# Gate and value projections by Strassen's seven products, in a transformer block whose weights stream through one core

## The chip, the cores and the metric

One core of a Trainium2 (trn2) chip runs the whole program. The metric is the device time of one execution in microseconds (us). Names used below: TensorE (PE) multiplies, VectorE (DVE) and ScalarE (ACT) work on tiles in the on-chip memory (SBUF) and on the accumulators (PSUM), GpSimd (POOL) and SyncE (SP) here hardly do more than start transfers from and to DRAM.

## What is computed

One layer of a decoder block on 256 positions of width 2048, in float32:

```python
h = rmsnorm(x, norm_g)
proj = einsum('bsd,df->bsf', h, w_in)          # 2048 -> 18432, cut into 14 pieces
(a_q, a_k, a_v, a_g, b_a, b_b, b_g, c_u, c_v, c_g, d_q, d_k, d_v, d_g) = split(proj)
ya = stick_breaking_attention(a_q, a_k, a_v) * silu(a_g)       # 8 heads of 128
yb = conformer_conv(b_a, b_b, ...) * silu(b_g)                 # gated, 31 taps, layer norm, silu
yc = spatial_gating(gelu(c_u), gelu(c_v), ...) * silu(c_g)     # layer norm, 128x128 mixing
yd = dilated_mixture(d_q, d_k, d_v) * silu(d_g)                # 8 heads, 3 patterns
yproj = einsum('bsnc,ncd->bsnd', [ya, yb, yc, yd], w_branch)   # 1024 -> 2048 each
gates = sigmoid(einsum('bsd,df->bsf', h, w_gate) + b_gate)     # 2048 -> 4 x 2048
merged = sum(gates * yproj, branch)
out = rmsnorm(x + merged @ w_out, final_g)
```

## The kernel before

All weights lie in DRAM as tiles of 128 x 2048 floats (1 MB), in the order of use; `load_weights` takes the next one through SP's queue into one of three `st` buffers. A float32 product is made of three matmuls in TensorE's rounded format: ScalarE copies the tile to `hi` in that format, VectorE subtracts to get the rest, `lo` (`split`, lines L130 and L131, in halves of 1024 columns, five buffers each of `hi` and `lo`), and hi·hi, hi·lo, lo·hi are added up in PSUM. The normed input stands in SBUF all the time as `xhl`, its hi beside its lo.

Two forms of projection use this. `mm_t` gives a transposed result (128 columns of the projection by 256 positions): for each of 16 slices of the depth one matmul of 512 columns (`xhl` hi and lo side by side) and one of 256 (L245, L248). `mm_n` gives positions by 512 columns: 24 matmuls of 512 columns for each tile (L286 to L288). `proj_t` does two transposed tiles (a unit) and evacuates them: ScalarE copies one half, VectorE adds the other (L266, L267).

The work goes: d_v and the norm of x (`make_h`); b_a and b_b; the eight heads of d, where `conv` puts the 248 steps of the convolution ("taps", L412) behind the units as filler; `conv_norm`; then for each branch in the order d, b, a, c the function `gate_proj`: four times, sixteen tiles of the branch's gate (two times 512 columns in PSUM `psg`, with a bias matmul, four tiles a chunk), a sigmoid, and two tiles of the branch's projection (`psy`), multiplied and added to `merged` in SBUF. Between the gates stand the units of b_g, of a (a_v, heads) and of c (c_v, c_u with c_g). At the end `out`.

What must wait for another engine is put off: `later(n, fn)` puts a step on a list, `tick()`, at the end of each unit, counts down and runs those due. So the scores of a head stand behind the next unit, its softmax's transposes behind the one after, then its values; `flush` empties the list. A branch's result `y` is kept in SBUF, as hi and lo (`put_y`).

The order of instructions on every engine is set by the framework's scheduler, which starts from the code's order and moves instructions by priority: weight splits by `SPLIT_AHEAD` = 300 ahead, taps by 100 back.

## Time and profile before

| | |
|---|---|
| median of 3 runs | 1505.48 us (1505.38 to 1506.88) |
| profiled execution | 1508.27 us, span of its profile 1506.6 us |
| mean granted clock of TensorE | 0.994 |
| TensorE matmuls busy | 1479.1 us, 98% of the span |
| VectorE busy | 944.4 us, 63% |
| ScalarE busy | 760.2 us, 50% |
| GpSimd busy | 10.2 us, 1% |
| read from DRAM / written | 277.18 MB / 2.10 MB, 185 GB/s over the span |
| weight tiles loaded whole through SP | 254 of 1 MB, median 4.8 us each |

The busy time of an engine is the time in which it has an instruction at work; in the rows of a line a name such as `lo<-st,hi` says what is written from what, with buffer numbers left out. VectorE's busy share is an average: the page's forty slices go from 4 tenths to 9.

The program by time: to 50 us d_v and the norm; to 145 b_a and b_b; to 506 the heads of d; to 610 the gate and projection of d; then b_g and the gate of b; from about 640 a_v and the heads of a; the gate of a from 1017; c from 1120; the gate of c from 1270; `out` from 1406.

### The profile page before, as it was taken

To read this page: it belongs to the slowest core of one execution; us is meant where nothing else is said; L and a number is where in the kernel's file an instruction comes from. 1 tells how busy PE (TensorE), PEld (TensorE's weight loads), DVE (VectorE), ACT (ScalarE), POOL (GpSimd) and SP (SyncE) were. 2 spreads that over 40 slices of the span, in tenths; PEclk is the share of its full clock that TensorE was granted. 3 is DMA by queue.
4 is the path that set the end of the run, shared out by engine and by line. 5 is a ranking of instruction groups with operands and counts; after the bars stand their busy time and mean duration, and the time that the engine had idled before them with its cause. 6 is when DMAs were issued, how large, how long until landed. Compare 5 with 4: busy or idle time off the path is not lost.

```text
span 1506.6 us, 18648 instructions
## 1 busy us (share of the span) xinstructions
PE 1479.1 (98%) x7484; PEld 1255.4 (83%) x7484; DVE 944.4 (63%) x1249; ACT 760.2 (50%) x860; POOL 10.2 (1%) x22
## 2 busy tenths in 40 slices
PE   7999999999999999999999999999999999999997
PEld 5888888888888788888888888887888888888786
DVE  8899999866566754555545455554545666555454
ACT  7644445564454644454444466654444667444352
POOL 0000000000000000000000000000000000000000
PEclk9999999999999999999999999999999999999999
DMA  8555554445444555555555545444555555555562
GB/s 302 211 195 184 180 187 177 169 166 191 173 168 170 201 203 186 192 195 189 186 186 195 194 168 172 168 177 154 196 195 195 181 183 198 200 190 177 192 217 84
DMA packets 41318, 280.47 MB, mean 186 GB/s; under 512 B 4784, under 2 KB 4784, under 8 KB 8592
## 3 DMA queue, kind: packets, MB, share of 16 engines
q1 hardware_dynamic: 38880, 272.00, 50.5%
q0 software_dynamic: 1632, 6.24, 1.3%
q8 instruction: 58, 0.95, 0.3%
q10 hardware_dynamic: 720, 1.06, 0.2%
q14 instruction: 28, 0.23, 0.0%
HBM read 277.18 MB, written 2.10 MB: 185 GB/s over the span
## 4 chain that ended last, share of the span: by engine, by line
PE 97%; ACT 1%; DVE 1%; DMA 1%; issue 0%; DVEq 0%; ACTq 0%
PE ps L245 30%; PE ps L248 15%; PE psg L286 8%; PE psg L288 8%; PE psg L287 8%; PE psy L286 4%; PE psy L288 4%; PE psy L287 4%; PE psn L287 3%; PE psn L288 3%; PE psn L286 3%; PE pso L286 2%; PE pso L287 2%; PE pso L288 2%; DMA xt<-in_xT_dram 0%; PE psg L369 0%
## 5 line engine op out<-in xcount | busy, mean ns | idle before, releaser
L131 DVE TENSOR_TENSOR lo<-st,hi 128x1024 fp32r<-128x1024 f32 (+1 forms) x506 | 616.0, 1219 | 460.7 <-ACT hi L130 459.2
L130 ACT ACTIVATE hi<-st 128x1024 fp32r<-128x1024 f32 (+1 forms) x506 | 533.4, 1056 | 671.7 <-PE ps L245 262.3
L245 PE MATMUL ps<-xhl,hi 128*128 128x512 f32 x1920 | 675.5, 398 | 0.0
L248 PE MATMUL ps<-xhl,lo 128*128 128x256 f32 x1920 | 519.5, 281 | 0.0
L245 PEld LDWEIGHTS ps<-xhl,hi 128*128 128x128 f32 x1920 | 355.2, 188 | 74.6
L248 PEld LDWEIGHTS ps<-xhl,lo 128*128 128x128 f32 x1920 | 362.3, 189 | 9.6
L286 PE MATMUL psg<-hi,xhl 128*128 128x512 f32 x512 | 201.0, 393 | 1.1 <-ACT hi L130 1.1
L288 PE MATMUL psg<-hi,xhl 128*128 128x512 f32 x512 | 200.3, 391 | 0.0
L287 PE MATMUL psg<-lo,xhl 128*128 128x512 f32 x512 | 200.2, 391 | 0.0
L286 PEld LDWEIGHTS psg<-hi,xhl 128*128 128x128 f32 x512 | 96.4, 188 | 21.6 <-ACT hi L130 1.7
L288 PEld LDWEIGHTS psg<-hi,xhl 128*128 128x128 f32 x512 | 96.6, 189 | 20.2
L287 PEld LDWEIGHTS psg<-lo,xhl 128*128 128x128 f32 x512 | 96.6, 189 | 20.0
L412 DVE SCALAR_TENSOR_TENSOR cv<-glu,vec_sb,cv 128x255 f32<-128x255 f32 (+26 forms) x240 | 100.8, 463 | 0.2
L286 PE MATMUL psy<-hi,y 128*128 128x512 f32 x256 | 99.6, 389 | 0.0
L287 PE MATMUL psy<-lo,y 128*128 128x512 f32 x256 | 99.6, 389 | 0.0
L288 PE MATMUL psy<-hi,y 128*128 128x512 f32 x256 | 99.6, 389 | 0.0
L288 PEld LDWEIGHTS psy<-hi,y 128*128 128x128 f32 x256 | 48.1, 188 | 10.0
L287 PEld LDWEIGHTS psy<-lo,y 128*128 128x128 f32 x256 | 48.1, 188 | 10.0
L286 PEld LDWEIGHTS psy<-hi,y 128*128 128x128 f32 x256 | 48.1, 188 | 9.9
L286 PE MATMUL psn<-hi,xhl 128*128 128x512 f32 x128 | 49.8, 389 | 0.0
L287 PE MATMUL psn<-lo,xhl 128*128 128x512 f32 x128 | 49.8, 389 | 0.0
L288 PE MATMUL psn<-hi,xhl 128*128 128x512 f32 x128 | 49.8, 389 | 0.0
(207 smaller groups left out, 1105.2 us busy)
## 6 DMA issues: line engine op xcount, KB each, us to landing
st<-in_w_dram SPq DMA_DIRECT2D x254, 1024.0 KB, 4.8
xr<-in_x_dram POOLq DMA_DIRECT2D x8, 256.0 KB, 3.9
xt<-in_xT_dram SPq DMA_DIRECT2D x3, 512.0 KB, 8.7
st<-in_w_dram SPq DMA_DIRECT2D x4, 256.0 KB, 5.3
st<-in_w_dram SPq DMA_DIRECT2D x2, 512.0 KB, 7.4
fg<-in_final_g_dram POOLq DMA_DIRECT2D x1, 1024.0 KB, 6.8
out_dram<-r SPq DMA_DIRECT2D x4, 256.0 KB, 3.2
out_dram<-r ACTq DMA_DIRECT2D x4, 256.0 KB, 3.5
```

The source lines that it names most:

```text
L130: A.activation(hi, src, AF.Copy)
L131: V.tensor_sub(lo, src, hi.bitcast(F32))
L245: T.matmul(ps[:, j, :], hi[:, o:o + P], rhs[:, k, :], start=start, stop=stop)
L248: T.matmul(ps[:, j, 0:S], lo[:, o:o + P], rhs[:, k, 0:S], start=False, stop=False)
L286: T.matmul(ps[:, tb, :], lh(k0 + kk, 0, tb), hi[:, o:o + 512], start=st, stop=False)
L287: T.matmul(ps[:, tb, :], lh(k0 + kk, 0, tb), lo[:, o:o + 512], start=False, stop=False)
L288: T.matmul(ps[:, tb, :], lh(k0 + kk, 1, tb), hi[:, o:o + 512], start=False, stop=sp)
L412: V.scalar_tensor_tensor(dst, src, wc, dst, op0=ALU.mult, op1=ALU.add)
```

## The change

Strassen's algorithm (in its form with 15 additions) multiplies two matrices cut in 2 x 2 blocks with seven block products instead of eight, for some additions of blocks beforehand and of products after. Here the left matrix is the normed input, cut in two halves of 128 positions and two of 1024 of depth; its four sums `s1`, `s2`, `s3`, `n4` are made once (`make_sx`) and split to hi and lo. The right one is a piece of 2048 x 1024 of a gate's weights, or the whole of a_v's or c_v's. `group` makes seven products of two half products each; a half product is one weight tile with twelve matmuls of 512 columns into one PSUM bank (`X`, `Z`, `Y`). Sums of weight tiles are made on VectorE before the split (`add_to`, eight to a group). A group loads twelve tiles, four of them for the second time, in place of eight. There are eight groups for the gates and two for values.

A group is a generator: `step(n)`, called between the weight tiles of other units, runs the next n half products of the first group in `queue`. Gate d and a_v's groups run beside the last head of d and the units of b_g, those of gates b and a beside branch d and the units of a, c_v and gate c beside branches b and a and the units of c. A gate's result goes to DRAM (`g_dr`) after its sigmoid and comes back in `branch`, the remaining half of `gate_proj`. The results `y` (`y_dr`) and the merged sum (`m_dr`) go through DRAM too. Each y is loaded back whole through SP's queue (`yf`) and split there.

Weight tiles are split whole, 2048 wide, into three `hi` and two `lo` buffers; there are six `st` buffers. And TensorE no longer follows the scheduler (`manual_schedule`): its instructions stand in the order of the code. The other engines are still scheduled, with `SPLIT_AHEAD` = 100.

```diff
-SPLIT_AHEAD = 300
+SPLIT_AHEAD = 100
...
-    st_p = ctx.enter_context(tc.tile_pool(name="st", bufs=3))
-    sp_p = ctx.enter_context(tc.tile_pool(name="sp", bufs=5))
...
+    st_p = ctx.enter_context(tc.tile_pool(name="st", bufs=6))
+    hi_p = ctx.enter_context(tc.tile_pool(name="hi", bufs=3))
+    lo_p = ctx.enter_context(tc.tile_pool(name="lo", bufs=2))
+    so_p = ctx.enter_context(tc.tile_pool(name="so", bufs=5))
+    ps_x = ctx.enter_context(tc.tile_pool(name="psx", bufs=1, space=bass.MemoryType.PSUM))
+    ps_n = ctx.enter_context(tc.tile_pool(name="psn", bufs=2, space=bass.MemoryType.PSUM))
+    ps_t = ctx.enter_context(tc.tile_pool(name="pst", bufs=3, space=bass.MemoryType.PSUM))
...
+    ctx.enter_context(tc.manual_schedule(engines={mybir.EngineType.PE}))
...
     def tick():
...
         for fn in due:
-            fn()
+            with tc.high_priority(SPLIT_AHEAD):
+                fn()
...
     def make_h():
...
-        pp = ps_2.tile([P, 2, 512], F32, tag="a2", name="pp")
-        pst, psn = pp[:, 0, :], pp[:, 1, :]
+        pst = ps_s.tile([P, 512], F32, tag="s", name="pst")
+        psn = ps_s.tile([P, 512], F32, tag="s", name="psn")
...
+    def proj_t(e0, e1, funcs=(None, None), n=0):
+        dst = qk_p.tile([P, 2, S], F32, tag="qk", name="dst")
+        for j, e in enumerate((e0, e1)):
+            ps = ps_t.tile([P, 512], F32, tag="t", name="ps")
+            mm_t(ps, next_weights(e), xhl)
...
+            step((n + 1) // 2 if j == 0 else n // 2)
+        tick()
+        return dst
...
+    def make_sx():
+        def quarter(k0, t0, name):
+            q = st_p.tile([P, KB, P], F32, tag="st", name=name)
...
...
+        V.tensor_sub(a22[:], a21[:], a22[:])
+        put("s1", a22[:])
+        V.tensor_sub(a22[:], a22[:], a11[:])
+        put("s2", a22[:])
...
+    def group(expect, sink, bias=None):
...
+        def half(ps, st, name, j, first, last):
+            lh = x_part(name)
+            hi, lo = split_tile(st)
+            for kk in range(4):
+                k, o = 4 * j + kk, kk * 512
+                for i, (part, w_) in enumerate(((0, hi), (0, lo), (1, hi))):
+                    T.matmul(ps[:], lh(k, part), w_[:, o:o + 512], start=first and j == kk == i == 0,
...
+        def add_to(st, other):
+            with tc.high_priority(SPLIT_AHEAD):
+                V.tensor_add(st[:], st[:], other[:])
...
+        X = ps_x.tile([P, 512], F32, tag="x", name="X")
...
+        for j in range(2):
+            ts.append(tile_of(0, 0, j))
+            half(X, ts[j], "a11", j, bias is None, True)
+            yield
+        p1 = keep(X, "p1")
+        Z = ps_n.tile([P, 512], F32, tag="n", name="Z")
...
+        for j in range(2):
+            add_to(ts[j], tile_of(1, 0, j))
+            half(Z, ts[j], "s1", j, bias is None, True)
+            yield
+        p5 = keep(Z, "p5")
+        for j in range(2):
+            add_to(ts[j], tile_of(1, 1, j))
+            half(X, ts[j], "s2", j, False, True)
+            yield
+        u2 = keep(X, "u2")
+        for j in range(2):
+            t3, b22 = tile_of(1, 0, j), tile_of(1, 1, j)
+            add_to(t3, b22)
+            half(Z, b22, "n4", j, False, True)
+            yield
+            half(X, t3, "s3", j, False, True)
...
+        Y = ps_n.tile([P, 512], F32, tag="n", name="Y")
+        for j in range(2):
+            b21 = tile_of(0, 1, j)
+            add_to(ts[j], b21)
+            half(Y, b21, "a12", j, True, True)
+            yield
+            half(X, ts[j], "a22", j, False, True)
...
+        done(0, 0, V.tensor_add, Y, p1, p1)
+        done(1, 0, None, X, X, X)
...
+    def put_y(b, h, n, src):
+        nc.gpsimd.dma_start(y_dr[b][:, h:h + n, :], src)
+
+    def branch(b, first=False, sink=None, n=0):
+        yf = st_p.tile([P, 2048], F32, tag="st", name="yf")
+        nc.sync.dma_start(yf[:], y_dr[b][:].rearrange("p k t -> p (k t)"))
+        yhl = [phase(n, F32R) for n in ("yh", "yl")]
+        with tc.high_priority(SPLIT_AHEAD):
+            split(yhl[0][:], yhl[1][:], yf[:])
...
+        for c in range(4):
+            psy = n_banks(1 if queue else c, "psy")
+            for q in range(2):
+                mm_n(psy, next_weights(("brN", bi, c, q)), 4 * q, y_lh, q == 0, q == 1)
+                step(n)
+            tick()
+            for tb in range(2):
+                nc.gpsimd.dma_start(g[:], g_dr[bi, tb, :, o:o + 512])
+                V.tensor_mul(g[:], psy[tb][:], g[:])
...
+                    nc.gpsimd.dma_start(m[:], m_dr[tb, :, o:o + 512])
+                    V.tensor_add(g[:], g[:], m[:])
+                if sink is None:
+                    nc.gpsimd.dma_start(m_dr[tb, :, o:o + 512], g[:])
...
+    for h0 in range(0, NH, 2):
+        sg = proj_t(ft("d_g", h0), ft("d_g", h0 + 1), (AF.Silu, AF.Silu))
+        conv(8)
+        if h0 == 6:
+            conv(len(taps))
+            conv_norm()
+            queue += [gate_group("d", 0), gate_group("d", 1), v_group("a_v", AF.Copy)]
+        d_head(h0, sg, 0)
+        d_head(h0 + 1, sg, 6 if h0 == 6 else 0)
...
+        bg = proj_t(ft("b_g", i), ft("b_g", i + 1), (AF.Silu, AF.Silu), n=6)
...
     for h0 in range(0, NH, 2):
         a_pair(h0)
+    while queue:
+        step()
+        tick()
+    while pending:
+        tick()
+    queue += [v_group("c_v", AF.Gelu_apprx_tanh), gate_group("c", 0), gate_group("c", 1)]
+    branch("b", n=1)
+    branch("a", n=1)
...
+        ug = proj_t(ft("c_u", i), ft("c_g", i), (AF.Gelu_apprx_tanh, AF.Silu), n=3 if i < 6 else 4)
+        later(2 if i < 6 else 1, lambda i=i, ug=ug: c_mix(i, ug))
+    while queue:
+        step()
+        tick()
+    while pending:
+        tick()
...
+    branch("c", sink=sink_c)
```

Three places in the order of instructions. First, the end of the first head of d. On ScalarE, before, between the split of the last d_q and d_k (`e3`) and the exponentials of the softmax (`e0`, `e1`, line L443 of before, L546 of after) there stand two half-tile splits `hi`; `bt` is an evacuation:

```order
L130 ACTIVATE e3_1880<-dst_1867 128x512
L130 ACTIVATE hi_2045<-st_2039 128x1024
L130 ACTIVATE hi_2119<-st_2117 128x1024
L266 ACTIVATE bt_1980<-ps_1884 128x512
L443 ACT_TABLE_LOAD
L443 ACTIVATE e0_1323,sm_1325<-e0_1323,sm_1325 128x384
L443 ACTIVATE e1_1324,sm_1325<-e1_1324,sm_1325 128x768
```
```order
L94 ACTIVATE qh_1774<-dst_1663 128x512
L233 ACTIVATE bt_1818<-ps_1779 128x256
L94 ACTIVATE hi_1933<-st_1931 128x2048
L233 ACTIVATE bt_1860<-ps_1821 128x256
L94 ACTIVATE hi_1999<-st_1997 128x2048
L546 ACT_TABLE_LOAD
L546 ACTIVATE ph_d0_1258,sm_1356<-ph_d0_1258,sm_1356 128x384
L546 ACTIVATE ph_d1_1259,sm_1356<-ph_d1_1259,sm_1356 128x768
L559 ACTIVATE ph_d0_1258<-pp_1863 128x384
```

In the new order the second evacuation of a unit and one whole-tile split stand ahead of the table load and the exponentials, and the copy of the transposed weights follows at once. On TensorE at the same place (`po`, `pp` are the transposes of the softmax's result, `s` the scores of the next head, `ps` transposed tiles):

```order
L245 MATMUL ps_2116<-xhl_107,hi_2165 128x512
L245 MATMUL ps_2224<-xhl_107,hi_2227 128x512
L455 MATMUL po_1855<-cst_sb_99,e0_1323 128x128
L248 MATMUL ps_2224<-xhl_107,lo_2228 128x256
L456 MATMUL po_1855<-cst_sb_99,e1_1324 128x128
L457 MATMUL po_1855<-cst_sb_99,e1_1324 128x128
```
```order
L210 MATMUL ps_1821<-xhl_119,hi_1824 128x512
L556 MATMUL pp_1863<-cst_sb_109,ph_d0_1258 128x128
L557 MATMUL pp_1863<-cst_sb_109,ph_d1_1259 128x128
L558 MATMUL pp_1863<-cst_sb_109,ph_d1_1259 128x128
L530 MATMUL s_1868<-dst_1663 128x128
L532 MATMUL s_1868<-qh_1774 128x256
L533 MATMUL s_1868<-ql_1775,qh_1774 128x256
L534 MATMUL s_1868<-qh_1774,ql_1775 128x256
L210 MATMUL ps_1888<-xhl_119,hi_1891 128x512
```

Before, the transposes stand among the matmuls of a later unit; now they stand between the last matmul of one unit and the first of the next, with the scores behind them.

Second, VectorE: before in a gate (here gate b), now in a unit of the last head of d with half products beside it. L131 and L95 are splits, L384 and L385 the multiplication by the gate and the merging, L333 the sums of weight tiles, L234 an evacuation:

```order
L131 TENSOR_TENSOR lo_5929<-st_5926,hi_5928 128x1024
L131 TENSOR_TENSOR lo_5933<-st_5926,hi_5932 128x1024
L384 TENSOR_TENSOR gt_5816<-psy_5818,gt_5816 128x1024
L131 TENSOR_TENSOR lo_5963<-st_5960,hi_5962 128x1024
L385 TENSOR_TENSOR merged_4459<-merged_4459,gt_5816 128x2x512
L131 TENSOR_TENSOR lo_5967<-st_5960,hi_5966 128x1024
```
```order
L333 TENSOR_TENSOR st_4052<-st_4052,st_4135 128x2048
L95 TENSOR_TENSOR lo_4078<-st_4034,hi_4077 128x2048
L95 TENSOR_TENSOR lo_4097<-st_4094,hi_4096 128x2048
L333 TENSOR_TENSOR st_4034<-st_4034,st_4156 128x2048
L95 TENSOR_TENSOR lo_4139<-st_4052,hi_4138 128x2048
L333 TENSOR_TENSOR st_4052<-st_4052,st_4175 128x2048
L333 TENSOR_TENSOR st_4261<-st_4261,st_4263 128x2048
L95 TENSOR_TENSOR lo_4160<-st_4034,hi_4159 128x2048
L234 TENSOR_TENSOR dst_3989<-ps_4093,bt_4132 128x256
L95 TENSOR_TENSOR lo_4179<-st_4052,hi_4178 128x2048
```

Between the splits of the half products stand the sums of weight tiles, as wide as a whole split, one or two at a time.

Third, the end of c. SP's queue in its last part, before and after, and TensorE there (`pz` is the spatial mixing of c, `psg` the gate of c before, `X` the last half product of gate c after):

```order
L203 DMA xt<-in_xT_dram 128x1024
L214 DMA cst_sb<-in_cst_dram 128x784
L124 DMA st<-in_w_dram 128x2048 x253
L685 DMA out_dram<-r 128x512 x4
L761 UNCONDITIONAL_BRANCH
```
```order
L88 DMA st<-in_w_dram 128x2048 x16
L455 DMA yf<-y_dr_a 128x2048
L88 DMA st<-in_w_dram 128x2048 x52
L455 DMA yf<-y_dr_c 128x2048
L88 DMA st<-in_w_dram 128x2048 x24
```
```order
L617 MATMUL pz<-swb,vc 128x128 x4
L369 MATMUL psg<-bgr,sel 128x512 x2
L286 MATMUL psg<-hi,xhl 128x512
L287 MATMUL psg<-lo,xhl 128x512
L288 MATMUL psg<-hi,xhl 128x512
```
```order
L328 MATMUL X<-hi,xhl 128x512 x2
L328 MATMUL X<-lo,xhl 128x512
L328 MATMUL X<-hi,xhl 128x512
L729 MATMUL pz<-swb,c_v 128x128 x6
L250 MATMUL psy<-hi,yh 128x512
L251 MATMUL psy<-lo,yh 128x512
L252 MATMUL psy<-hi,yl 128x512
```

The three last mixes now stand behind the last half product, and the projection of c, which needs their result by way of DRAM, follows them; in SP's queue the load of that result stands ahead of the last 24 weight tiles.

## The prediction

> **What bounds the kernel now.** I read the page first: the busy line, the forty slices, the chain that ended last.

> ```profile
> span 1506.6 us, 18648 instructions
> PE 1479.1 (98%) x7484; PEld 1255.4 (83%) x7484; DVE 944.4 (63%) x1249; ACT 760.2 (50%) x860; POOL 10.2 (1%) x22
> DVE  8899999866566754555545455554545666555454
> GB/s 302 211 195 184 180 187 177 169 166 191 173 168 170 201 203 186 192 195 189 186 186 195 194 168 172 168 177 154 196 195 195 181 183 198 200 190 177 192 217 84
> PE 97%; ACT 1%; DVE 1%; DMA 1%; issue 0%; DVEq 0%; ACTq 0%
> ```

> TensorE is the bound nearly everywhere: all its idle time is 1506.6 − 1479.1 = 27.5 us, and the chain is its own work for 97%. A removed matmul is therefore worth its full pitch, and every new wait of TensorE costs its full length. But VectorE's average of 63% hides stages, so I cut the trace by stage, then asked what TensorE waits for.

> ```profile
> 145.00:250.00 105.00, 105.00 (x607) 91.74 (x607) 99.47 (x191) 53.18 (x62) 0.00 (x0) 1.00 0.52 185
> 506.00:610.00 104.00, 101.27 (x440) 83.10 (x439) 52.70 (x47) 49.72 (x53) 2.26 (x3) 0.98 0.55 197
> 1017.00:1120.00 103.00, 101.63 (x443) 83.83 (x444) 51.31 (x44) 43.95 (x42) 0.00 (x0) 0.98 0.50 179
> ```
> ```profile
> PE psn L286 <- ACT xuh L209: 5.9, 1, 5.9
> PE pt L642 <- DVE merged L385: 3.7, 1, 3.7
> PE psg L369 <- ACT gt L375: 3.7, 2, 1.8
> ```

> The first fence has a row for each stage: its ends and length, then the busy time of PE, weight load, DVE, ACT and POOL, the granted clock, the share of DMA and its GB/s. The second has TensorE's waits: total, times, longest. From 145 to 250 (first dilated heads, convolution taps as filler) DVE is full, yet PE never waits: the taps could be put off. In the gates (506, 1017) DVE is half idle. The change spends that idle half, and the question is whether it lies where the new work lands.

> **The change part by part.** *Matmuls removed.* The order shows 3024 matmuls of 512 columns in place of 3264, and 16 bias matmuls in place of 32. Pitch, first and last of 24 rows:

> ```profile
> 600.12 0.39 PE L286 MATMUL psg<-hi,xhl 128*128 128x512 f32 x1
> 605.33 0.39 PE L288 MATMUL psg<-hi,xhl 128*128 128x512 f32 x1
> 302.39 0.40 PE L245 MATMUL ps<-xhl,hi 128*128 128x512 f32 x1
> 303.80 0.40 PE L245 MATMUL ps<-xhl,hi 128*128 128x512 f32 x1
> ```

> 5.21/23 = 0.2265 us, so 256 × 0.2265 = **−58.0**. A transposed pair takes 1.41/4 = 0.352; a transposed tile (16 pairs) 5.6 us, a 24-matmul tile 5.44, a half product of a group (12) 2.72.

> *Waits that go.* The gates at 506 and 1017 leave 104.0−101.3 = 2.7 and 103.0−101.6 = 1.4 idle, most of it the two waits of 1.8 for a sigmoid, which held the first matmul of the next PSUM pair; groups no longer have that pair. The 3.7 ahead of the last transposes goes too: `turn(3)` now has three output tiles in front of it. **−7.8**. These waits also cost clock:

> ```profile
> 509.86 0.73 PE L369 MATMUL psg<-bgr,sel 128*128 128x512 f32 x2 [1.83 <-ACT gt L375]
> 511.00 0.63 PE L286 MATMUL psg<-hi,xhl 128*128 128x512 f32 x1
> 513.56 0.63 PE L286 MATMUL psg<-hi,xhl 128*128 128x512 f32 x1
> 1408.83 0.63 PE L287 MATMUL pso<-lo,mh 128*128 128x512 f32 x1
> 1411.39 0.63 PE L287 MATMUL pso<-lo,mh 128*128 128x512 f32 x1
> 1406.66 1.94 PE L642 MATMUL pt<-cst_sb,merged 128*128 128x128 f32 x8 [3.68 <-DVE merged L385]
> 1346.15 1.03 PE L642 MATMUL pt<-cst_sb,merged 128*128 128x128 f32 x8
> 22.76 0.50 PE L287 MATMUL psn<-lo,xuh 128*128 128x512 f32 x1 [1.64 <-DVE lo L131]
> ```

> After 1.83 us idle the pitch is (513.56−511.00)/6 = 0.427 for seven matmuls, 7×0.2 = 1.4 lost. After 3.68 it stays so for about nine, 1.8, and the eight transposes take 1.94 where others take 1.03, 0.9: 2.7. After 1.64 the first matmul takes 0.50 and no slow ones follow. The stage at 1017 has the same clock as that at 506 (0.98), so its wait counts as the first: 1.4+1.4+2.7 = **−5.5** that goes.

> *What VectorE gets.* Its prices:

> ```profile
> 29.04 3.49 DVE L131 TENSOR_TENSOR lo<-st,hi 128x1024 fp32r<-128x1024 f32 x3
> 510.47 2.29 DVE L502 TENSOR_TENSOR cv<-cv,mean 128x2048 f32<-128x2048 f32 x1
> L385 DVE TENSOR_TENSOR merged<-merged,gt 128x1024 f32<-128x1024 f32 x12 | 14.6, 1220 | 0.0
> L267 DVE TENSOR_TENSOR dst<-ps,bt 128x512 f32<-128x512 f32 x60 | 41.0, 684 | 0.0
> 164.40 2.03 DVE L412 SCALAR_TENSOR_TENSOR cv<-glu,vec_sb,cv 128x253 f32<-128x253 f32 x5
> 36.01 1.75 DVE L183 RECIPROCAL rstd<-rs 128x256 f32<-128x256 f32 x1
> 38.75 0.42 DVE L187 TENSOR_TENSOR rs<-rstd 128x256 f32<-128x256 f32 x1
> 42.76 6.42 DVE L230 SCALAR_TENSOR_TENSOR xt<-xt,vec_sb,rstd 128x256 f32<-128x256 f32 x16
> L485 DVE TENSOR_REDUCE red<-csq 128x256 f32<-128x2048 f32 x1 | 3.9, 3920 | 0.0
> ```

> Instructions overlap by about 0.08 (three of 1.22 in 3.49), so a 2048-wide split or add is 2.21, a 1024-wide one 1.14, a tap 0.39. A group has 14 splits, 8 adds and three 512-wide drains: 22×2.21 + 2 = 50.7 us of VectorE beside 14×2.72 = 38.1 of TensorE. Alone it would put VectorE 12.6 behind. What stands between repays: two transposed tiles leave 11.2 − 2×2.21 − 0.8 (evacuation) = 6.0. `lo` has two whole-tile buffers, so VectorE is at most two tiles ahead, and what it falls behind in a lump can't be worked off beforehand.

> *Convolution norm to the end of b_g* (18 transposed tiles, 42 half products, which are three groups). TensorE: 18×5.6 + 42×2.72 + 5.6 of small matmuls = 220.6. VectorE: 61 splits 134.8, 24 adds 53.0, and 53: two reductions 7.8, norm 8, `make_sx` 13.7 (eight 1024-wide steps, four splits), evacuations and drains 13.7, b_g and the last heads 10; 240.8 in all. By sums +20. Walking the order tile by tile (a `lo` starts when the tile two earlier is used, a tile when its `lo` is there) gives 253.7, +33. The lump is where norm and `make_sx` stand, 59 us of VectorE beside 40 of TensorE. At two group boundaries the next group's first matmul also waits for the sigmoid that empties the single `X` buffer (table and drain), 1.5 each, +3. **+36**; ends 20 and 45.

> *a units* (24 transposed tiles, 48 half products): TensorE 275, VectorE 247 (72 splits, 28 adds, softplus and evacuations). Enough by sum; but where an add stands between two splits the second comes 2×2.21 = 4.4 after the first, the tile between covers 2.7 and the lead some 0.5: 1.2 late, eight times. **+9** (0 to 41, see the rivals). *Branches d, b, a*, 131 against 122, the first split of each late: **+4** (0 to 13). *c units*: the layer norm puts 25.5 us of VectorE beside a first unit of 19.6, and one more lump like it late: **+7** (0 to 25).

> *Places where code order takes TensorE's cover away.* Other prices:

> ```profile
> L499 ACT ACTIVATE csq<-cv x1: 1919/1919/1919, 493.1 to 493.1; 128x2048 f32<-128x2048 f32 x1
> L627 ACT ACT_TABLE_LOAD x8 | 10.3, 1283 | 0.1
> L548 ACT ACTIVATE sp<-sp 128x768 f32<-128x768 f32 x4 | 3.4, 846 | 0.0
> L628 ACT ACTIVATE dst<-dst 128x256 f32<-128x256 f32 x8 | 3.3, 418 | 0.1
> st<-in_w_dram SPq DMA_DIRECT2D x254, 1024.0 KB, 4.8
> xr<-in_x_dram POOLq DMA_DIRECT2D x8, 256.0 KB, 3.9
> out_dram<-r SPq DMA_DIRECT2D x4, 256.0 KB, 3.2
> xt<-in_xT_dram SPq DMA_DIRECT2D x3, 512.0 KB, 8.7
> ```

> - Start: pst and psn now follow each other before the next product. Square-root table 1.28, root 0.42, reciprocal 1.75, five small steps 1.9 and one split between, 7.1; then 6.42 of scaling and four 1024-wide splits before the next `lo`, 2.3 more than its cover. **+9.4** (7 to 12).
> - First head: transposes stand right behind one unit. After its last matmul: evacuation 0.42, a split 1.92 that stands ahead on ScalarE, table 1.28, two exponentials 1.5, on VectorE small steps 1.8 and ten taps 3.9: 10.8. Then 38 taps (14.8) ahead of the next split beside 11.7 of matmuls, 2.7, and 1.9 earlier. **+15.4**. The second head, 3.8 more. Later heads have no taps: there the same chain is shorter than the unit it stands beside. Ends 8 (the taps done early) and 25.
> - End of a heads: `while pending` leaves nothing between the last scores, sums and values. ScalarE: three tables 3.8, five 768-wide steps 4.2; VectorE: the masked scores 2×0.5, two 768-wide steps 0.9 each, two subtractions 0.5: 12.6, less half a unit's rest. **+12**; the weights of branch b are split meanwhile.
> - End of c: three mixes behind the last product, then six small matmuls 1, nine VectorE steps 3.3, the store (3.2 to 3.9) 4, the 1 MB `yf` 4.8, its two splits and the next tile's 1.92+1.92+2.2. **+19**. Before, these mixes had the next gate's products in front of and behind them. On SP all 24 weight loads left stand behind `yf`, whose issue waits for the stores; on POOL the stores stand behind the load of `fg` and a gate's store, and branch c's 16 loads behind the stores. Ends 14 (both transfers at 3.2, one split hidden) and 29 (both near 8.7).

> *Elsewhere the trips through DRAM cost nothing:* `yf` of d, b and a is loaded several tiles after its stores, a gate's sums long before its branch; six `st` buffers and five `so` buffers are the cover. If it goes, up to 10 us (one transfer of 3.2 to 8.7 exposed). y's own splits go from 20 small ones to four of 2048: VectorE's work there stays about the same. About 40 MB more weights and 36 MB of y, gates and sums on 280 make some 230 GB/s; the first slice shows 302, six `st` buffers cover: 0.

> *Clock.* Eleven new waits of 1.8 us or more. The rows above lose 0 after 1.64, 1.4 after 1.83, 2.7 after 3.68. Seven short ones at 0.7 and four long (two heads' ends, a, c) at 2.7: **+15**, ends 0 and 30. [...]

> **Sum.** −58.0 −7.8 −5.5 = −71.3. Added: 36+9+4+7+9.4+15.4+3.8+12+19 = 115.6, and 15. Net +59.3: span 1565.9. The profiled execution is 1.7 above its span and 2.8 above the median of the runs, so **1565 us**.

> **Rivals.**
> - *VectorE keeps ahead* (other side). For it: 145 to 250, 99.5 of 105 busy without a wait. Against: there the work between could be put off, adds cannot. Of the 115.6, about 69 is VectorE-paced; without it 47 stays, with 11 of clock: 1506.6−71.3+58−1.1 = **1492**. It decides where the VectorE-paced waits come below 71.3−58 = 13 us.
> - *VectorE paces every Strassen stage* as the walk has it in the first, 253.7/220.6 = 1.15: a units +41 for 9, c 163×0.15 = 25 for 7: **1615**. For it: the same group everywhere. Against: a and c units have 10% of VectorE to spare.
> - *The clock falls after each short wait.* Some 25 further waits near 1.2 us, 1.4 each: **1600**. Against: the row at 22.76, without slow matmuls after 1.64 us. [...]
> - *It doesn't do what it says*: excluded, the order has 240 fewer products.

> **How the numbers follow.** Forecast 0.60 (its own range 1530 to 1595: stretch 20 to 45, clock 0 to 30, c end 14 to 29); VectorE ahead 0.13; pacing everywhere 0.12; clock 0.06; and 0.09 for VectorE-paced waits half as long, 1506.6−71.3+47+35+12−1.1 = 1528 and, with the clock at 0 and the c end at 14, 1511. 0.2%, 3 us, is about what a measurement of this kernel can tell from no change. Faster takes the first rival and a little of the last, 0.14; same 0.03; slower 0.83. The range 1510 to 1612 leaves out the first rival and half of the pacing one.

> **What would show it.** In the changed profile: PE near 1420 busy by its pitch with idle over 100; the chain with DVE at 5% or more instead of 1%; waits of `ps`, `X` and `Z` on `lo` and `hi`; one long wait each at `pp`, `cc`, and the first `psy` of branch c. Wrong it would be if these rows total under 70 us, if `lo` waits are missing from the stretch after the heads, or if `psy` in branch c waits under 10.

## The result, and the profile after

The changed kernel takes 1633.49 us (median of 4 runs, 1629.29 to 1635.42), the one before 1505.43 beside it: a ratio of 1.0845, 95% interval 1.0821 to 1.0868. Slower, as forecast, but by 128 us and not by 60; the time lies above the range.

The page of the changed kernel, the lines that answer to those of before (the clock in tenths stands in the fourth):

```profile
span 1633.1 us, 18440 instructions
PE 1470.6 (90%) x7228; PEld 1229.5 (75%) x7228; DVE 1255.0 (77%) x1256; ACT 877.8 (54%) x798; POOL 85.7 (5%) x161
DVE  7699998555789998896787888875768888745554
PEclk9999989999989999999999999997989999988999
PE 44%; DVE 7%; DMA 5%; issue 2%; ACT 2%; POOL 0%; DVEq 0%; SPq 0%; ACTq 0%; POOLq 0%
```

TensorE idles 162 us in place of 27, and is busy 1470.6, only 8.5 less than before, though it has 58 us of matmuls fewer. Most of that is the clock: its mean is 0.956 for 0.994, and where every slice of the row before shows 9 tenths, here 6 slices show less. The time that the low clock costs is worked out in the next section: 37 us more than before. TensorE's waits (total, times, longest):

```profile
PE ps L213 <- DVE lo L95: 27.2, 17, 4.7
PE psy L250 <- ACT hi L94: 24.8, 1, 24.8
PE pp L556 <- DVE ph_d L551: 15.3, 2, 11.7
PE X L328 <- DVE lo L95: 11.3, 10, 2.1
PE psy L251 <- DVE lo L95: 10.2, 6, 4.7
PE cc L668 <- ACT pr_a L94: 7.7, 1, 7.7
PE psn L199 <- DVE rstd L156: 6.4, 1, 6.4
PE s L530 <- DVE dst L566: 6.4, 1, 6.4
```

The stages (length; busy PE, weight load, DVE, ACT, POOL; clock; DMA share; GB/s): start, b_a to the heads of d, the stretch from the convolution norm to the end of b_g, branch d, a units with the end of a, branches b and a, c units, and from the end of c on.

```profile
0.00:67.50 67.50, 51.02 (x200) 40.37 (x201) 51.64 (x65) 39.67 (x49) 2.58 (x9) 0.95 0.73 279
67.50:448.60 381.10, 366.38 (x2107) 320.18 (x2106) 300.99 (x527) 175.74 (x194) 1.09 (x2) 0.98 0.45 160
448.60:714.50 265.90, 238.64 (x1145) 197.35 (x1144) 236.92 (x191) 169.19 (x155) 11.35 (x21) 0.95 0.69 254
714.50:789.20 74.70, 69.61 (x292) 56.25 (x290) 48.89 (x28) 31.26 (x21) 7.03 (x13) 0.95 0.70 249
789.20:1116.90 327.70, 293.40 (x1448) 244.72 (x1446) 262.20 (x167) 212.62 (x178) 13.53 (x25) 0.96 0.66 239
1116.90:1272.70 155.80, 141.94 (x580) 114.16 (x580) 117.90 (x86) 68.15 (x42) 25.24 (x47) 0.93 0.78 272
1272.70:1454.70 182.00, 170.69 (x860) 142.86 (x858) 147.92 (x107) 121.20 (x108) 11.21 (x19) 0.98 0.59 217
1454.70:1633.10 178.40, 138.91 (x609) 113.58 (x608) 88.54 (x90) 59.99 (x54) 13.63 (x26) 0.90 0.57 203
```

No stage is free of idle time or at full clock. VectorE is busy 77%, in the stretch 89% (236.9 of 265.9), elsewhere 81% at most: it isn't a plain bound either.

### The profile page after: what moved, and what is told of

Same layout as the page of the kernel before. It is cut to its first block, busy times and chain, and to the rows that moved or that the text cites. A ratio compares the mean times of both kernels' runs of the same rounds, so it can differ in the third digit from the quotient of the medians.

```text
span 1633.1 us, 18440 instructions
## 1 busy us (share of the span) xinstructions
PE 1470.6 (90%) x7228; PEld 1229.5 (75%) x7228; DVE 1255.0 (77%) x1256; ACT 877.8 (54%) x798; POOL 85.7 (5%) x161
## 4 chain that ended last, share of the span: by engine, by line
PE 44%; DVE 7%; DMA 5%; issue 2%; ACT 2%; POOL 0%; DVEq 0%; SPq 0%; ACTq 0%; POOLq 0%
PE ps L210 9%; PE X L328 9%; PE ps L213 5%; DVE lo L95 5%; PE Z L328 4%; PE psy L251 3%; PE psy L252 3%; PE psy L250 3%; DMA st<-in_w_dram 2%; PE Y L328 2%; PE pso L250 2%; PE pso L252 2%; PE pso L251 2%; DMA gl<-g_dr 1%; DVE st L333 1%
## 5 line engine op out<-in xcount | busy, mean ns | idle before, releaser
L95 DVE TENSOR_TENSOR lo<-st,hi 128x2048 fp32r<-128x2048 f32 (+2 forms) x318 | 712.9, 2248 | 215.1 <-issue 77.9
L94 ACT ACTIVATE hi<-st 128x2048 fp32r<-128x2048 f32 (+2 forms) x318 | 596.9, 1881 | 249.7 <-PE psy L252 91.4
L213 PE MATMUL ps<-xhl,lo 128*128 128x256 f32 x1920 | 524.8, 284 | 27.2 <-DVE lo L95 27.2
L333 DVE TENSOR_TENSOR st<-st 128x2048 f32<-128x2048 f32 x80 | 182.7, 2286 | 47.6 <-DMA st<-in_w_dram 47.2
L250 PE MATMUL psy<-hi,yh 128*128 128x512 f32 x256 | 106.4, 416 | 31.5 <-ACT hi L94 24.8
L251 PE MATMUL psy<-lo,yh 128*128 128x512 f32 x256 | 106.4, 416 | 10.5 <-DVE lo L95 10.2
L252 PE MATMUL psy<-hi,yl 128*128 128x512 f32 x256 | 105.8, 413 | 5.8 <-DVE yl L95 5.8
L328 PE MATMUL X<-hi,xhl 128*128 128x512 f32 x320 | 106.2, 396 | 4.6 <-ACT g L429 4.2
L328 PE MATMUL X<-hi,s 128*128 128x512 f32 x320 | 106.8, 397 | 0.0
L513 DVE SCALAR_TENSOR_TENSOR cv<-glu,vec_sb,cv 128x235 f32<-128x235 f32 (+26 forms) x240 | 98.3, 464 | 0.2
L328 PE MATMUL X<-lo,s 128*128 128x512 f32 x160 | 65.0, 407 | 11.3 <-DVE lo L95 11.3
## 6 DMA issues: line engine op xcount, KB each, us to landing
st<-in_w_dram SPq DMA_DIRECT2D x294, 1024.0 KB, 5.0
gl<-g_dr POOLq DMA_DIRECT2D x32, 256.0 KB, 5.8
m_dr<-gl POOLq DMA_DIRECT2D x24, 256.0 KB, 5.6
ml<-m_dr POOLq DMA_DIRECT2D x24, 256.0 KB, 6.4
g_dr<-p POOLq DMA_DIRECT2D x16, 256.0 KB, 4.2
g_dr<-u POOLq DMA_DIRECT2D x8, 256.0 KB, 4.3
g_dr<-g POOLq DMA_DIRECT2D x8, 256.0 KB, 4.1
xr<-in_x_dram POOLq DMA_DIRECT2D x8, 256.0 KB, 4.6
```

Source lines behind the costliest of these rows:

```text
L94: A.activation(hi, src, AF.Copy)
L95: V.tensor_sub(lo, src, hi.bitcast(F32))
L213: T.matmul(ps[:, 0:S], lo[:, o:o + P], rhs[:, k, 0:S], start=False, stop=False)
L250: T.matmul(ps[tb][:], lh(k0 + kk, 0, tb), hi[:, o:o + 512], start=st, stop=False)
L251: T.matmul(ps[tb][:], lh(k0 + kk, 0, tb), lo[:, o:o + 512], start=False, stop=False)
L252: T.matmul(ps[tb][:], lh(k0 + kk, 1, tb), hi[:, o:o + 512], start=False, stop=sp)
```

## The experiments

The account below uses three numbers of each trace. *Idle* is the sum of TensorE's listed waits; some 6 us ahead of the first matmul are among them in every kernel. *Clock* is half of the time in which TensorE worked while the trace's clock record showed half rate. *Work* is what is left of the span, less the 9 us after the last matmul.

| kernel | time | span | idle | clock | work |
|---|---|---|---|---|---|
| before | 1505.4 | 1506.6 | 18 | 5.8 | 1473 |
| changed | 1633.5 | 1633.1 | 153 | 42.4 | 1429 |
| thin sums | 1563.0 | 1561.2 | 107 | 22.4 | 1423 |
| ordinary products | 1604.5 | 1602.8 | 96 | 22.4 | 1476 |
| cover at two places | 1617.1 | 1615.4 | 137 | 39.8 | 1429 |
| four waits kept busy | 1616.1 | 1614.4 | 101 | 25.8 | 1479 |
| TensorE scheduled | 1590.2 | 1588.5 | 116 | 25.4 | 1439 |
| ordinary, scheduled | 1543.7 | 1541.9 | 48 | 10.5 | 1475 |
| scheduled, c covered | 1576.6 | 1574.9 | 97 | 31.7 | 1437 |
| ordinary, scheduled, c covered | 1518.9 | 1517.1 | 27 | 5.4 | 1475 |
| scheduled, c covered, thin sums | 1511.6 | 1509.9 | 57 | 15.4 | 1429 |
| scheduled, c covered, one load | 1552.9 | 1551.2 | 85 | 21.6 | 1436 |
| scheduled, c covered, thin sums, one load | 1504.1 | 1502.4 | 51 | 15.7 | 1427 |
| sums on GpSimd | 1770.7 | 1768.9 | 241 | 84.9 | 1434 |

All but before and changed are single runs. The times of these two are medians, their spans those of the profiled executions, which took 1508.3 and 1634.9. Beside the others the kernel before took 1505.7 to 1506.9 (in one case the median of 15 runs from 1503.6 to 1508.4). The changed kernel's own runs spread by 6 us, so differences under some 5 us between single runs are not read.

**Thin sums.** Is VectorE the cause? The sums keep their places and waits but cost little:

```diff
-                V.tensor_add(st[:], st[:], other[:])
+                V.tensor_add(st[:, 0:64], st[:, 0:64], other[:, 0:64])
```

> The eighty sums of two weight tiles are made over 64 of their 2048 columns only (the numbers of the gates and of a_v and c_v are then others); the loads, the order in the code and all waits for two tiles stay. It takes some 80 x 2.15 = 172 us of work from VectorE. Theory 1 (idle and clock come from three sources: code order at five places, loads and trips through DRAM in the branches, and VectorE only in the stretch after the heads, the a units and the c units): the lo waits of the stretch, the a units and the c units go with the half-rate periods behind them, some 40 to 60 us, so 1575 to 1595. Theory 2 (VectorE paces everything; the other waits are its shadows): over 100 us go, 1530 or less. Theory 3 (loads pace it: six st buffers are too few for 1 MB tiles of which two are held): less than 20 us go, 1615 or more.

1563.0, 70 us less: a little more than theory 1 allowed, far less than theory 2 asked. Of it 46 are idle and 20 clock. What stays shows in its waits, the same handovers as before the edit:

```profile
PE psy L250 <- ACT hi L94: 22.9, 1, 22.9
PE pp L556 <- DVE ph_d L551: 15.3, 2, 11.7
PE cc L668 <- ACT pr_a L94: 7.7, 1, 7.7
PE psn L199 <- DVE rstd L156: 6.4, 1, 6.4
PE s L530 <- DVE dst L566: 6.2, 1, 6.2
PE ps L213 <- DVE lo L95: 4.7, 3, 2.4
```

The first five, 58.5 us, hardly see the sums (60.6 before the edit); the `lo` wait of transposed tiles falls from 27.2 to 4.7.

**Ordinary products in the new frame.** How much of the loss is Strassen's at all?

```diff
-        X = ps_x.tile([P, 512], F32, tag="x", name="X")
...
+        for c in range(2):
+            ps = [ps_x.tile(...), ps_n.tile(...)]
...
+            for q in range(4):
+                hi, lo = split_tile(load_weights(expect(c, q)))
+                for tb in range(2):
...
+                yield
```

(With eight steps to a group for fourteen, the numbers of steps beside the units are lowered to match.)

> The same program (manual TensorE order, y, gates and sums through DRAM, gates and values beside other units, the same buffers) with ordinary products in place of Strassen's: eight tiles to a group, each used for both halves of the positions, no sums of tiles, no tile loaded twice, 256 matmuls more, 58 us. make_sx still runs. Theory 1: the handovers by code order (start, two heads, end of a, end of c, some 65 us idle) and most of their clock stay, VectorE's waits and most load waits go: 1633 + 58 - 45 - 25, 1600 to 1640, far above the kernel before, so most of the loss is not Strassen's. Theory 2 (VectorE, loaded by the sums, is the cause): about the time of before plus the start, 1520 to 1550. Theory 3 (loads): 40 MB fewer, 1560 to 1590.

1604.5, within theory 1's range. So 98 of the 128 us come from the frame (code order, trips through DRAM, buffers), and Strassen adds 29 on top: 47 us of work less, 57 of idle and 20 of clock more. These two shares hold for this order of the code only: with most of the frame's waits gone, further below, Strassen adds 58.

**Cover at the end of a and of c.** Fewer steps beside the last units, so that half products are left for the ends:

```diff
-            qk = proj_t(ft("a_q", h0 + j), ft("a_k", h0 + j), n=4)
+            qk = proj_t(ft("a_q", h0 + j), ft("a_k", h0 + j), n=2 if h0 == 6 else 4)
...
-        ug = proj_t(..., n=3 if i < 6 else 4)
+        ug = proj_t(..., n=2)
```

> Strassen as in the change; only the numbers of steps differ: two half products for four in each unit of the last pair of a heads, and two for three or four in the units of c, so that six and ten half products are left for the loops at the ends, where ticks run between them. The scores, sums and values at the end of a and the way of y_c through DRAM then have half products beside them. Theory 1 (these two places cost their own waits, 12.8 and 24.8 us, and 13 to 15 us of clock behind them): 35 to 50 us less, 1583 to 1598. Rival (the leftover half products run at VectorE's pace, 50.7 for 38.1 a group, and give it back, or the chain only moves behind them): 1615 to 1640.

1617.1, 16 less: in the rival's range, though the theory was right at one place. The wait of 24.8 before the first `psy` of branch c is gone. At the end of a the wait of `cc` became longer:

```profile
PE psy L251 <- DVE lo L95: 18.0, 8, 5.2
PE cc L668 <- ACT pr_a L94: 10.9, 1, 10.9
```

On ScalarE a split of 1.91 and the sigmoid of a gate with its table load (1.28 + 0.63) now stand between the steps of this chain, from the half products left over; and `psy` waits 18.0 for `lo` over all branches, not 10.2 (in b and a 12.0, not 3.7).

**The clock by itself.** Runs of 64 matmuls with a wait of set length between:

```diff
+        ps = psp.tile([P, 512], F32, tag="p", name="p")
+        for i in range(n):
+            T.matmul(ps[:], lh[:], g[:, 0:512], start=i == 0, stop=i == n - 1)
+        A.activation(g[:, 0:512], ps[:], AF.Copy, scale=1e-3)
+        for w in widths:
+            A.activation(g[:, 0:w], g[:, 0:w], AF.Copy)
```

> Only the clock: 64 matmuls of 512 columns, then a wait of TensorE for ScalarE of a length set by the width of a copy (about 1 to 3 us in ten sizes, twice each; then some 5, 9, 17 and 26 us), then 64 more; and at the end rows of short waits every 12, 24, 36 and 48 matmuls. Nothing of the block is computed. Theory 1 (each wait of about 1.9 us or more is followed by half rate for 3.4 us or a multiple): no half-rate period up to 1.8 us, one behind each longer wait, and none in the rows of short waits of 1 to 1.5 us. Rival a (only gaps over some 3 us count): none behind waits of 2 to 3 us. Rival b (short waits add up): half rate in the rows of short waits too.

None of the three held. Of two waits of 1.83 us one is followed by half rate and one is not; of the eight waits from 2.05 to 2.69 only one is; rows of waits of 0.75 to 1.51 every 12 to 48 matmuls never are. The half-rate periods begin and end on a grid of 3.41 us (in the changed kernel's trace they begin 56, 70, 121 and so on up to 465 steps of 3.4133 us behind the first, none off by more than 0.001 us, and last 1, 2, 3, 6 or 8 steps), and what told the waits apart was the idle time within one window of the grid. Both waits of 1.83 and one of 2.47, then the windows around the first two (length; busy PE, weight load, ACT, POOL; clock):

```profile
187.83 14.80 PE L33 MATMUL p<-g,lh 128*128 128x512 f32 x64 [1.83 <-ACT g L36]
204.46 1.78 PE L33 MATMUL p<-g,lh 128*128 128x512 f32 x4 [1.83 <-ACT g L36]
291.18 1.20 PE L33 MATMUL p<-g,lh 128*128 128x512 f32 x4 [2.47 <-ACT g L36]
```
```profile
184.32:187.73 3.41, 1.67 (x8) 1.05 (x6) 1.61 (x2) 0.00 (x0) 1.00 0.00 0
187.73:191.14 3.41, 3.31 (x15) 2.74 (x16) 0.05 (x1) 0.00 (x0) 1.00 0.02 5
201.39:204.80 3.41, 1.58 (x8) 0.99 (x6) 1.65 (x2) 0.00 (x0) 1.00 0.00 0
204.80:208.21 3.41, 3.41 (x10) 2.64 (x9) 0.00 (x0) 0.00 (x0) 0.50 0.00 0
```

The first wait runs from 186.00 to 187.83 and crosses the border at 187.73: 1.73 in its window, full rate after. The second, 202.63 to 204.46, lies in one window whole: half rate for the next. The 2.47 at 291.18 is cut at 290.13 in 1.42 and 1.05: nothing. In the traces of before and of the change the same holds: half rate begins behind each window with 1.84 us of listed waits or more, and behind none with 1.74 or less (for the first 9 to 10 us these traces have no record of the clock); it ends behind the first window with little idle (0.41 let it up, 0.61 did not). Several waits in one window add up: in the kernel with TensorE scheduled, 1.09 and 0.96 together brought half rate. The rows of short waits never put that much into one window. Over all kernels here a few windows between 1.2 and 1.9, and below 0.6, go the other way; why stays open; gaps too short to be listed come to under 1 us in any whole trace. So one wait under 1.7, alone in its window, mostly cost no clock here; one of 2 to 3 did or did not by its place (one of the eight above, all five in the changed kernel), and of 101 waits over 3 in these traces 98 did; the three others were under 3.2 long. A little over half a window idle was enough: 1.83 of 3.41 in the second wait above, 1.84 in the trace of before.

**The four long waits kept busy.** Does the clock cost what the account says?

```diff
+    def keep_busy(ps, n):
+        for _ in range(n):
+            T.matmul(ps[:], xhl[:, 0, 0:P], xhl[:, 1, :], start=True, stop=True, skip_group_check=True)
...
+            keep_busy(pp, {0: 48, 5: 14}.get(h, 0))
...
+            keep_busy(psy[0], 105 if b == "c" and c == 0 else 0)
```

> The changed kernel with matmuls that nobody reads put into four of TensorE's long waits (48 at the first head's transposes, 14 at the sixth's, 30 and 14 at the end of a, 105 at the end of c), each a little shorter than the wait it stands in, so that the waits' ends stay where they are and only the clock differs. Theory (a window of 3.41 us on a fixed grid with 1.8 us or more idle is followed by half rate until a window with at most half a us idle): the half-rate time behind these waits, 1.8 + 1.7 + 4.5 + 2.2, goes: 1620 to 1627. Rival (the clock is no separate cost; the matmuls behind a wait would have waited for VectorE anyway): 1631 to 1637.

1616.1: 17 us less by doing 211 matmuls (47.8 us) more. The clock's loss falls from 42.4 to 25.8, which is the whole gain; the half-rate periods go from 19 to 13. It is more than the 10 forecast: some later waits, too, have no period behind them now, though they are as long. That part is put down to their place in the grid; no run shows it alone.

**TensorE's order left to the scheduler**, with Strassen and without:

```diff
-    ctx.enter_context(tc.manual_schedule(engines={mybir.EngineType.PE}))
```

> The changed kernel with one line gone, the one that makes TensorE follow the order of the code; its instructions are again placed by the scheduler. Theory (the waits at the start, at the heads' transposes, at the scores behind the convolution norm and at the end of a, 6 + 18 + 6 + 13 us, come from code order, with 10 to 15 us of half rate behind them): 40 to 55 us less, 1578 to 1595; the 25 us at the end of c stay. Rival (the chains behind them are as long in any order, and VectorE's lumps decide): 1615 to 1640.

> The ordinary products of the second experiment, with TensorE's order left to the scheduler. The run with code order took 1604.5, 97.6 more than before. Theory: the same 45 us of waits and 10 to 15 of half rate go, 1540 to 1560; what is left over before (1507) is the end of c with 25 to 28 us, the waits of branches for gates that come from DRAM, about 10, and their clock. Rival (the loss lies in whole-tile splits with two lo buffers and in the way through DRAM, not in the order): 1585 or more.

1590.2 and 1543.7: 43 and 61 us less, theory in both. The 11.7 at `pp`, the 7.7 and 4.2 at the end of a and the 6.4 at the start are gone from the scheduled kernel's waits (of `pp` one of 2.3 is left, of `cc` 1.0); at the top stands the end of c, then splits:

```profile
PE psy L249 <- ACT hi L93: 24.6, 1, 24.6
PE psy L250 <- DVE lo L94: 14.4, 8, 4.9
PE ps L212 <- DVE lo L94: 13.6, 15, 2.7
PE X L327 <- ACT hi L93: 12.7, 8, 4.7
```

**Both with the end of c covered**, and the sums thin once more:

> The changed kernel with TensorE's order left to the scheduler (1590.2 alone) and two half products for three or four in the units of c, so that ten are left for the loop at the end of c. Theory (the end of c costs 25 us idle and some clock for want of cover, in either order): 20 us less, 1566 to 1575. Rival (the scheduler's order has already found that cover, or the half products left over run at VectorE's pace and take it back): 1583 to 1592.

> Ordinary products, TensorE's order left to the scheduler (1543.7 alone), and branch a runs without steps, so that eight tiles of gate c are left for the end of c. Theory (of the 38 us that this kernel stands above the one before, the end of c is 25 to 30): 1510 to 1520, the rest being waits for gates out of DRAM, the start and the second VectorE lumps. Rival (the 38 us lie in whole-tile splits and the trips through DRAM): 1533 or more.

> As the first of these, and the sums of weight tiles over 64 of 2048 columns (gates, a_v and c_v come out with other numbers): what Strassen's 58 us could bring if the sums cost nothing. Theory (sums cost 70 us by VectorE): 1495 to 1512, at or a little below the kernel before and below plain products with the same cover. Rival (the loads, twelve tiles for eight, take VectorE's place): 1530 or more.

Ordinary products: 1518.9, 25 less, as forecast; the frame is then 12 to 13 us above before. Strassen: 1576.6, 14 less, between theory and rival. With thin sums 1511.6, at the end of theory's range: still not below the kernel before. In this frame Strassen costs 58 over ordinary products (29 in the order of the code), and if its sums cost next to nothing it gains 7 of the 58 us of matmuls that it saves.

**Second loads.** Of the 51 that stay, are the four tiles that each group loads twice the cause? The first four sums of a group add the tile to itself (the first two are shown; the next two lose `tile_of(1, 1, j)` in the same way):

```diff
-            add_to(ts[j], tile_of(1, 0, j))
+            add_to(ts[j], ts[j])
```

> Strassen, TensorE scheduled, end of c covered (1576.6), but the first four sums of a group add a tile to itself, so that no tile is loaded twice: eight loads a group, eight sums still (gates, a_v and c_v come out with other numbers). Theory (second loads and the wait for two tiles in six buffers cost 25 to 50 us, in either state of the sums): 1530 to 1552. Rival (VectorE's work alone paces the groups, a tile that comes early waits for it): 1568 or more.

> The same with the sums over 64 of 2048 columns (1511.6 with all loads). Theory: 25 to 45 us less, 1467 to 1487, near plain products less 58 (1461), which would mean that loads were the rest. Rival (the rest is the group's own: one X bank that must be emptied before the next group, three more drains, short waits that refill TensorE): 1500 or more.

1552.9 with full sums, 24 less (0.9 above the theory's range, far from the rival's); 1504.1 with thin ones, 7.5 less (the rival). So the second loads cost much where VectorE has the full sums to do, and little where it has time to spare. 43 us of Strassen's lost gain remain with neither: against ordinary products 23 more of idle, 10 of clock and 10 of work, in some twenty waits of 0.5 to 4.7 us; 15 of the 51 us idle are for `hi`, of which a group has fourteen in place of eight. What each costs was not taken apart and stays open.

**The sums on GpSimd**, `nc.gpsimd.tensor_add` for `V.tensor_add`:

> The eighty sums of weight tiles on GpSimd in place of VectorE, the rest as in the change. No run has timed GpSimd at this. With thin sums VectorE's share came out as 70 us. Theory (VectorE's load by the sums is that share; GpSimd has 1550 us idle): if one sum takes up to 5 us there, 1565 to 1600. Rival (GpSimd is slower than the half product beside it, or slows VectorE, and its queue also holds the gates' stores and loads): 1640 or more.

1770.7, the rival. GpSimd's sums (first row), and VectorE's splits with them and, last, in the changed kernel:

```profile
L333 POOL TENSOR_TENSOR st<-st 128x2048 f32<-128x2048 f32 x80 | 403.8, 5049 | 347.3 <-DMA st<-in_w_dram 237.9 <-DVE lo L95 90.4 <-issue 15.6
```
```profile
L95 DVE TENSOR_TENSOR lo<-st,hi 128x2048 fp32r<-128x2048 f32 x308 | 887.3, 2888 | 310.5 <-PE ps L213 122.4 <-issue 107.4 <-PE pso L251 16.5
```
```profile
L95 DVE TENSOR_TENSOR lo<-st,hi 128x2048 fp32r<-128x2048 f32 x308 | 703.1, 2288 | 209.3 <-issue 77.9 <-PE ps L213 68.7 <-PE psy L251 18.0
```

A sum takes 5.05 us there for 2.29, 2.2 times as long, and longer than the half product (2.72) it stands in front of, and VectorE's splits grow from 2.29 to 2.89 on average, so that its 183 us of sums come back as 184 of splits.

The average hides two kinds. Of the 308 splits 224 overlap no sum, and none of these took over 2.30; the other 84 took 4.49 on average, up to 6.69. All 61 that begin while a sum runs end 2.15 to 2.16 us behind its end, as if they had begun there. A small split, which takes 0.69 in the changed kernel, shows it too:

```profile
494.37 4.65 POOL L333 TENSOR_TENSOR st<-st 128x2048 f32<-128x2048 f32 x1
496.07 3.51 DVE L95 TENSOR_TENSOR ql<-dst,qh 128x512 fp32r<-128x512 f32 x1 [1.53 <-ACT qh L94]
```

So in this trace the splits that began during one of GpSimd's sums behaved as if they waited for its end; the small one above ended 0.56 behind it.

**What the change is good for.** One part of it, the last transposes moved behind three tiles of the output product (`turn(3)`), put into the kernel before:

```diff
     gate_proj("c", yc, sink=sink)
-    flush()
...
+            if c == 0 and q == 3:
+                flush()
             mm_n(ps, next_weights(("out", c, q)), 4 * q, m_lh, q == 0, q == 3)
```

> The kernel before, with one thing taken from the change: the last transposes of the merged sum stand behind three tiles of the first output product and ahead of the fourth, where they are needed. Theory (the wait of 3.7 us and 2.7 us of half rate behind it go, nothing else moves): 1498.5 to 1500.5. Rival (the wait moves to the split of the transposes, in front of the fourth tile): 1503 to 1506.

1503.96 against 1506.44, ratio 0.9985 (0.9976 to 0.9994): below both kernels, by 0.15%, but by 2.5 us and not the 6 expected: that is the rival's range. In its profiled execution the span is 1501.2, 5.4 shorter, but there this kernel has one half-rate period and the kernel before three (1.6 us of clock for 5.8). That differs from run to run: the granted clock of the kernel before goes from 0.993 to 0.997 over its 15 runs. Of the wait of 3.7 one of 1.2 is left, for the split that the rival named:

```profile
PE pso L286 <- ACT mh L644: 1.2, 1, 1.2
```

## Why the prediction was right and wrong, step by step

Direction and mechanism held: gain of matmuls less than new waits. The sum was 67 us short (span 1633.1 for 1565.9). By the account: clock 27, idle 27, work 13.

- *Clock, +15: the step that failed most.* 42.4 were lost. Eleven waits were counted; half rate began behind 19. The four long ones (two heads' ends, a, c) lost 10.1, as priced (four times 2.7); the other fifteen periods lost 32.3, where seven at 0.7 stood in the sum. Short ones were priced from two rows (0 after 1.64, 1.4 after 1.83) as if the length decided. The window did: a period here lost 1.5 us or more, 2.2 on average, and where a wait ran on into the window of half rate, the next one could be at half rate too (behind the wait of 6.4 at `s` three windows were, for 3.1 us). The rival on the clock (1600) named the right term by a wrong mechanism, since in this trace no half rate began behind a window with 1.74 us idle or less; the one of 1615 came nearest in time, but VectorE didn't pace the a and c units as the stretch.
- *Products, −58.* Work went down by 45 against before and by 47 against ordinary products in the same frame. Some 12 us are lost again. They don't lie in gaps too short to be listed, which come to 0.4 us. TensorE stops 61 times for 11, and the last matmul of 512 columns before a stop is recorded with 0.39 us, where the pitch is 0.227: 50 times 0.16, some 8 us by this estimate. The rest stays open.
- *Branches, +4, and "loads and trips cost 0": wrong.* Branch d idles 5.0 and the first a unit 4.7, branches b and a 13.7. In the first two a weight tile is late in front of a sum, by 5.9 and 5.8 us. First VectorE's waits of this kind in the whole program, then the sum behind the 4.7 of branch d:

```profile
DVE st L333 <- DMA st<-in_w_dram: 47.2, 21, 5.9
```
```profile
757.39 2.29 DVE L333 TENSOR_TENSOR st<-st 128x2048 f32<-128x2048 f32 x1 [5.86 <-DMA st<-in_w_dram]
```

  VectorE idles 47.2 us for weight tiles, in front of sums. I had compared 230 GB/s with 302 and called six buffers the cover; a sum holds two of them and a group two more for most of its length, so a load starts late and its 5.0 us (the median here) show. That this is why the loads are late is argued; the edit on second loads, 24 us in the scheduled kernel, shows the size. The mean rate was 222.

  In branches b and a the trips show. The two longest waits, 4.2 each, stand behind a multiplication for which VectorE itself waited, 2.3 and 1.3 us, for a gate out of DRAM. The first:

```profile
1192.73 0.69 DVE L474 TENSOR_TENSOR gl<-psy,gl 128x512 f32<-128x512 f32 x1 [2.28 <-DMA gl<-g_dr]
1195.67 0.80 PE L252 MATMUL psy<-hi,yl 128*128 128x512 f32 x1 [4.21 <-DVE yl L95]
```

  The split of y stands behind that multiplication on VectorE. The gate had been stored some 80 us before; its load went out at 1184.8, on GpSimd's queue behind a store of the merged sum. A wait of 2.8 there stands behind a late weight tile again.
- *a units, +9*: 21.5 idle (34.3 of the stage less the 12.8 at the end of a), part of it the same waits for loads. *c units, +7*: 11.
- *Stretch, +36*: 27, of which 10 are not waits for splits but `pp` (3.6) and `s` (6.4, for the PSUM buffer that the sixth head's product waits in, behind the norm on VectorE). The bound from sums, 20, was the better number.
- *Start, heads, end of a, +9.4, 15.4, 3.8, 12*: measured 6.4 (just under its range), 11.7, 2.5, 12.8. These steps held, and the scheduled kernels show that it is the code order that makes them.
- *End of c, +19*: 24.8. VectorE's part was 2.2 us for 3.3, but the trips took 15.7 for 8.8, and a weight tile was late behind them:

```profile
1456.50 0.42 DVE L734 TENSOR_TENSOR dst<-dst 128x256 f32<-128x256 f32 x1
...
1458.96 0.54 POOL L449 DMA_DIRECT2D y_dr_c<-dst  x1 [1.14 <-DMA gl<-g_dr]
...
1465.65 0.33 SPq L455 DMA_DIRECT2D yf<-y_dr_c  x1
1466.08 16.05 SPq L88 DMA_DIRECT2D st<-in_w_dram  x7
...
1472.67 1.91 ACT L94 ACTIVATE yh<-yf 128x2048 fp32r<-128x2048 f32 x1 [18.99 <-DMA yf<-y_dr_c]
1477.54 1.91 ACT L94 ACTIVATE hi<-st 128x2048 fp32r<-128x2048 f32 x1 [2.96 <-DMA st<-in_w_dram]
1479.50 0.80 PE L250 MATMUL psy<-hi,yh 128*128 128x512 f32 x1 [24.79 <-ACT hi L94]
```

  The last of y is ready at 1456.9. Its store is issued at 1459.0, behind the loads of a gate and of `fg` on GpSimd's queue, and has landed at 1465.6; the load goes out then and lands at 1472.6; seven weight tiles are issued right behind it, which may be why it took 6.9. The first of these comes 3.0 after `yh` is done. The queue was named in the prediction, but no time was put to it. Behind it, branch c and `out` idle 5.7 more, for which the sum had no term.
- *Waits that go, −7.8 −5.5*: the one in front of the last transposes did, and is worth 0.15% by itself. The sigmoid's waits came back at the group boundaries (`X` on `g`, 4.2).
- *The rival on the other side*, VectorE ahead: dead. TensorE's waits for `lo` alone come to 58 us, far over the 13 that it allowed, and even with thin sums, the code order undone and the end of c covered the kernel stood at 1511.6.

## What to carry to other kernels

Where one engine is busy 98%, as TensorE was here, look at cover as well as at work (the work went down by 45 us, and the waits grew by 135): before counting removed matmuls, list for every chain between engines what runs beside it in the new order, and put a time to each queue that it passes. Price TensorE's waits with their clock, by windows of 3.41 us: one under 1.7 us, alone in its window, mostly cost nothing here; one over 3 us 1.5 to 3.1 on top, and 4.9 where three followed each other. Before fewer products are bought with sums of operands, ask whether the engine that sums, the loads that feed it and the buffers between have that time in the same stage: here VectorE and the loads had not (thin sums took 70 us off, the second loads left out 24); what the buffers alone cost was not tested.
